# Loads of w_ada issued by ScalarE instead of SyncE, in a decoder layer on one core

## The chip, the cores and the metric

The kernel runs on one core of a Trainium2 chip. The time is device microseconds of one launch. Three runs of the kernel before gave 1894.2, 1889.44 and 1890.69 us, median 1890.69. Engines: PE is TensorE (matmuls; PEld its weight loads), DVE VectorE, ACT ScalarE, POOL GpSimd, SP SyncE, which only issues DMAs here; a q behind an engine's name is its sequencer.

## The reference

One layer on x (1, 256, 4096) float32, with weights w_ada (4096 x 12288), w_in (4096 x 15520) and w_out (4096 x 4096):

```
mod = silu(c) @ w_ada + b_ada ;  shift, scale, gate = split(mod, 3)
h   = rms_norm(x, norm_g) * (1 + scale) + shift
z   = h @ w_in      -> uA, vA, gA, qB, kB, vB, gB, qI, kI, wI
yA  = chunked_sgu(uA, vA)            # gelu, layer_norm, 128x128 mixing per head
yB  = sparse_attention(qB, kB, vB, qI, kI, wI)   # top 64 keys per query, T5 bias
y   = concat(rms_norm(yA) * silu(gA), rms_norm(yB) * silu(gB)) @ w_out
out = x + gate * y
```

c is one vector, so that silu(c) @ w_ada is a product of a vector with a matrix of 201 MB: its cost is reading it.

## The kernel before

Every large product is done in float32 precision by splitting both factors into a high and a low part: a weight tile `raw` (two slices of 128 rows by 512 columns, 512 KB) is copied by ScalarE into high parts `whi` (line 419, two copies), and VectorE (line 425) and GpSimd (line 427) subtract these from `raw` into the low parts `wlo`. PE then multiplies high by high, high by low and low by high (line 457): 12 matmuls of 512 columns for a tile, 10 for the packed tiles of the indexer's queries, where two half products share one matmul.

The stream of weight tiles has 624 entries. First come eight blocks: a block is the four 128-row slices of w_in that belong to 512 features of h, against all columns that are needed early (23 groups of columns, two tiles each: 46 tiles, two of which are narrow, 160 columns). A block's partial products are added to groups in SBUF (line 829). Block b needs its 512 features of h, and these need shift and scale of the same features: a product of silu(c) with 4096 x 2 x 512 values of w_ada, in 32 tiles `wa` of 512 KB. While blocks 0 to 6 are multiplied, this product is made for the next block on VectorE: one `scalar_tensor_tensor` per `wa` tile adds csil[k] times the tile to a sum in PSUM (`ada_gemv`, lines 194 and 196), and `make_h` (lines 324 to 350) makes the features. The first block's product is made ahead of all this (`first_ada`, line 202). After the eighth block come eight visits of 16 tiles for the gate columns of w_in and eight for w_out, and beside them the layer norm, the mixing, the attention, and the product for `gate` (`make_gate`, line 939: 4 x 32 `wa` tiles, and one for the bias).

The order of every engine is the order in which the code is written, step by step. Step t (line 463) loads the raw tile of step t + 3 (`AHEAD`), splits tile t, flushes a delayed read, reads finished sums, lets work beside the stream advance (`tick`) and multiplies tile t. In the first seven blocks `pace(t)` is called ahead of step t and advances `all_h` by as many yields as are due: 33 a block, 32 of them a `wa` tile each.

There are four buffers for raw tiles (`WBUFS`) and two for `wa` tiles. All loads are issued by SyncE, each waiting there until its buffer is free. `ada_gemv` calls `load_ada` right after the operation that read a `wa` tile, so that the next load into that buffer stands in SyncE's order between the raw loads of two steps, and waits for that operation on VectorE.

Of the kernel before, what the change touches and what calls it, by code (L numbers as in the profile page):

```python
# [17 lines left out]
D = 4096  # L18
# [24 lines left out]
def layer(ctx, tc, x, c, w_ada, b_ada, norm_g, w_in, ln_v_g, ln_v_b, w_s, b_s, q_norm_g,  # L43
          k_norm_g, rel_bias, out_norm_a_g, out_norm_b_g, w_out, onehot, out):
    nc = tc.nc
# [20 lines left out]
    def after(read):  # L66
        pending.append(read)

    def flush():
        while pending:  # L70
            pending.pop(0)()

    def misc():
        while len(pending) > 1:
            pending.pop(0)()
        small_ones[0] += 1
        return ms.tile([P, 512], F32, name="ms_ps", tag="ms")

    def small(shape, name):
        return tiny.tile(shape, F32, name=name)  # L80
# [5 lines left out]
    w_ada_t = w_ada[0].rearrange("(k p) (s n) -> p k s n", p=P, s=3)  # L86
# [75 lines left out]
        ada_loads += [(k0, 1, 2, 1, 1024 * i_, 1024) for k0 in list(range(KC)) + [None]]  # L162
    ada_tiles = []

    def load_ada():
        if ada_loads:
            k0, per, s0, ns, d0, width = ada_loads.pop(0)
            wt = wp.tile([P, per, ns, width], F32, name="wa", tag="wa", bufs=2)
            if k0 == "norm":
                for a, src in enumerate((ln_v_g, ln_v_b)):  # L170
                    r = src[0:1, d0:d0 + 512]
                    nc.sync.dma_start(wt[:, 0, 0, a * 512:(a + 1) * 512],
                                      bass.AP(tensor=r.tensor, offset=r.offset, ap=[[0, P], [1, 512]]))
            elif k0 is None:
                nc.sync.dma_start(wt[0:1, 0, 0], b_ada[0:1, 2 * D + d0:2 * D + d0 + width])
            else:
                for kk in range(per):
                    nc.sync.dma_start(wt[:, kk], w_ada_t[:, k0 + kk, s0:s0 + ns, d0:d0 + width])
            ada_tiles.append(wt)

    def ada_gemv(ns, width):

        acc = ap.tile([P, 2, 512], F32, name="acc")
        flat = acc.rearrange("p a b -> p (a b)")
        per = 1024 // (ns * width)
        two = per == 2
        for k0 in range(0, KC, per):
            wt = ada_tiles.pop(0)
            for kk in range(per):
                k = k0 + kk  # L190
                src = wt[:, kk].rearrange("p s w -> p (s w)")
                dst = acc[:, k % 2] if two else flat
                if k < per:
                    nc.vector.tensor_scalar(dst, src, csil[:, k:k + 1], None, op0=OP.mult)
                else:
                    nc.vector.scalar_tensor_tensor(dst, src, csil[:, k:k + 1], dst,  # L196
                                                   op0=OP.mult, op1=OP.add)
            load_ada()
            yield
        return acc  # L200

# [160 lines left out]
    def tick():  # L362
        small_ones[0] = 0
        for b in list(beside):
            b[2] += b[1]
        for b in list(beside):
            if small_ones[0] > 1:
                break
            again = False
            while b[2] >= 1.0:  # L370
                b[2] -= 1.0
                if again:
                    flush()
                again = True
                if next(b[0], "end") == "end":
                    beside.remove(b)
                    break
# [22 lines left out]
    def load_w(t):  # L400
        if t >= len(stream) or t in raws:
            return
        v, i = stream[t]
        nk, w, c0 = min(2, len(v["ks"]) - i), v["w"], v["c0"]
        raw = wp.tile([P, 2, 512], F32, name="raw")
        raw = raw[:, :nk]
        nc.sync.dma_start(raw[:, :, :w], v["src"][:, v["ks"][i]:v["ks"][i] + nk, c0:c0 + w])
        raws[t] = raw
# [3 lines left out]
    def split(t):  # L412

        raw, w = raws.pop(t), stream[t][0]["w"]
        nk = raw.shape[1]
        hi = [sp.tile([P, 512], F32R, name="whi") for _ in range(nk)]
        lo = [sp.tile([P, 512], F32R, name="wlo") for _ in range(nk)]
        for kk in range(nk):
            nc.scalar.activation(hi[kk][:, :w], raw[:, kk, :w], AF.Copy)  # L419
        left = nk * pool_cols[0] * w // 1024 * 2  # L420
        for kk in range(nk):
            cut = w - min(left, w)
            left -= w - cut
            if cut:
                nc.vector.tensor_sub(lo[kk][:, :cut], raw[:, kk, :cut], hi[kk][:, :cut].bitcast(F32))  # L425
            if cut < w:
                nc.gpsimd.tensor_sub(lo[kk][:, cut:w], raw[:, kk, cut:w], hi[kk][:, cut:w].bitcast(F32))  # L427
        halves[t] = hi, lo
# [34 lines left out]
    def step(t):  # L463
        load_w(t + AHEAD)
        due = [v for u, v in reads if u <= t]
        del reads[:len(due)]
        split(t)
        flush()
        for v in due:
            v["read"](v)  # L470
        v, i = stream[t]
        if i == 0 and v["before"]:
            v["before"]()
        tick()
        multiply(t)
        if i + 2 >= len(v["ks"]):
            reads.append((t + 2, v))
# [311 lines left out]
    def norm_v():  # L789

        stats = small([P, NT, 4, 6], "stats")
        for g in range(4):
            z = groups[f"v{g}"]
            nc.scalar.activation(z, z, AF.Gelu_apprx_tanh)
            for n in range(NT):
                nc.vector.bn_stats(stats[:, n, g], z[:, n])
            yield
        mv = small([P, NT, 2], "mv")
        for n in range(NT):
            nc.vector.bn_aggr(mv[:, n], stats[:, n].rearrange("p a b -> p (a b)"))  # L800
        rv = small([P, NT], "rv")
        nc.vector.tensor_scalar(rv, mv[:, :, 1], EPS, None, op0=OP.add)
        nc.gpsimd.tensor_tensor(rv, rv, mhalf.to_broadcast([P, NT]), op=OP.pow)
        for g in range(4):
            z = groups[f"v{g}"]
            rows = ada_tiles.pop(0)[:, 0, 0]
            lg, lb = rows[:, :512], rows[:, 512:]
            for n in range(NT):
                nc.vector.scalar_tensor_tensor(z[:, n], z[:, n], mv[:, n, 0:1], lg,  # L809
                                               op0=OP.subtract, op1=OP.mult)  # L810
            yield
            for n in range(NT):
                nc.vector.scalar_tensor_tensor(z[:, n], z[:, n], rv[:, n:n + 1], lb,
                                               op0=OP.mult, op1=OP.add)
            load_ada()
            yield
        begin_gates()

# [120 lines left out]
    def make_gate(i):  # L939

        acc = yield from ada_gemv(1, 1024)
        tag = ("t4", "k", "vb", "t4")[i]
        accs = (t4 if tag == "t4" else zp).tile([P, 2, 512], F32, name="accs", tag=tag)
        nc.scalar.activation(accs, acc, AF.Copy)
        yield
        fl = accs.rearrange("p a b -> p (a b)")
        nc.vector.tensor_add(fl[0:1], fl[0:1], ada_tiles.pop(0)[0:1, 0, 0])
        load_ada()
        yield
        for a in range(2):  # L950
            hi = s2.tile([P, 512], F32R, name="ghi", tag="s2")
            lo = s2.tile([P, 512], F32R, name="glo", tag="s2")
            nc.scalar.activation(hi, accs[:, a], AF.Copy)
            nc.gpsimd.tensor_sub(lo, accs[:, a], hi.bitcast(F32))
            yield
            m = misc()
            nc.tensor.matmul(m, ones, hi, start=True, stop=False)
            nc.tensor.matmul(m, ones, lo, start=False, stop=True)

            def read(m=m, a=a):  # L960
                nc.scalar.activation(accs[:, a], m, AF.Copy)
                gates[2 * i + a] = accs[:, a]
            after(read)
        yield
# [3 lines left out]
    def all_gates():  # L968
        for i in range(4):
            yield from make_gate(i)  # L970
# [73 lines left out]
    def begin_gates():  # L1044
        nonlocal gat
        gat = later(GATE_STEPS, all_gates(), 234)
# [10 lines left out]
    first_h()  # L1057
    for t in range(AHEAD):
        load_w(t)
    load_ada()  # L1060
    load_ada()
    with tc.manual_schedule():
        for t in range(len(stream)):
            for begin in start.get(t, ()):
                begin()
            if t < last:
                pace(t)
            elif t == last:
                pool_cols[0] = POOL_REST
            step(t)  # L1070
        for _, v in reads:
            v["read"](v)
# [42 lines left out]
```

## Time and profile before

| | |
|---|---|
| three runs, median | 1890.69 us |
| the profiled execution's own time | 1893.78 us |
| its span, first to last instruction | 1892.1 us |
| PE, PEld busy | 1809.0, 1439.2 us |
| DVE, ACT, POOL busy | 1443.7, 933.4, 1299.2 us |
| mean granted TensorE clock | 0.994 |
| HBM read | 536.51 MB |

PE is busy for 96% of the span, but that is no measure of how well it is fed: matmuls overlap in the records, so that a row lasts longer than the distance between two starts. The idle time of PE in a stretch, and the distance of starts where nothing waits, say more. Waits are inferred from semaphores: the row `A <- B` sums the idle time of A's engine that ended when B was done. For SyncE, which is all sequencer, the wait is counted from the end of its last instruction.

### The profile page before, as it was taken

The numbers are of one execution on the slowest core, as the hardware profiler recorded it, in microseconds if no ns is written. First come the engines' busy times: TensorE is split into PE (matmuls) and PEld (weight loads), VectorE is DVE, ScalarE is ACT, GpSimd is POOL, SyncE is SP. The second block draws the span as 40 slices with busy tenths as digits, with TensorE's granted clock in tenths as the row PEclk, the third lists the DMA queues.
The fourth block names the chain that finished last, engine by engine and source line by source line (L and its number), as shares of the span: only waits on it lengthen the run. The fifth ranks groups of instructions, "written<-read, shape, count | busy, mean of one in ns | idle before, by whom it ended". The sixth has DMA issues, their size and how long they took to land.

```text
span 1892.1 us, 27366 instructions
## 1 busy us (share of the span) xinstructions
PE 1809.0 (96%) x8100; PEld 1439.2 (76%) x8100; DVE 1443.7 (76%) x1600; ACT 933.4 (49%) x1716; POOL 1299.2 (69%) x1340
## 2 busy tenths in 40 slices
PE   5798999999999999999999999999999999999998
PEld 2476777777777777787788877788888888888877
DVE  4656788888888888888777888887887577677744
ACT  4356445445454354444455556567654554544443
POOL 0366777777777776777785545767667777877786
PEclk9899999999999999999999999999999999999999
DMA  9899999999999989999975467886788799899974
GB/s 319 316 340 323 314 317 316 318 324 309 341 320 333 319 300 315 329 301 322 311 210 152 132 206 257 267 264 202 245 281 303 248 332 339 294 318 343 320 216 154
DMA packets 269550, 542.53 MB, mean 287 GB/s; under 512 B 17270, under 2 KB 25688, under 8 KB 269404
## 3 DMA queue, kind: packets, MB, share of 16 engines
q1 hardware_dynamic: 269404, 540.79, 84.5%
q8 instruction: 66, 1.08, 0.2%
q14 instruction: 80, 0.66, 0.1%
HBM read 536.51 MB, written 4.22 MB: 286 GB/s over the span
## 4 chain that ended last, share of the span: by engine, by line
PE 45%; DVE 2%; DMA 1%; POOL 1%; ACT 1%; issue 1%; SPq 0%; DVEq 0%; POOLq 0%; ACTq 0%
PE mm_ps L457 38%; PE ms_ps L457 2%; PE ms_ps L573 1%; DMA raw<-in_w_in_dram 1%; DVE wlo L425 1%; PE ms_ps L714 0%; DVE acc L196 0%; POOL wlo L427 0%; PE ms_ps L915 0%; PE ms_ps L867 0%; DVE v L809 0%; PE ms_ps L556 0%; PE ms_ps L742 0%; ACT whi L419 0%; DVE ix L585 0%
## 5 line engine op out<-in xcount | busy, mean ns | idle before, releaser
L427 POOL TENSOR_TENSOR wlo<-raw,whi 128x512 fp32r<-128x512 f32 (+1 forms) x1248 | 1220.8, 1004 | 543.8 <-ACT whi L419 467.0
L419 ACT ACTIVATE whi<-raw 128x512 fp32r<-128x512 f32 (+1 forms) x1248 | 730.9, 618 | 829.9 <-DMA raw<-in_w_in_dram 385.1
L425 DVE TENSOR_TENSOR wlo<-raw,whi 128x320 fp32r<-128x320 f32 (+2 forms) x624 | 636.7, 1022 | 317.3 <-ACT whi L419 200.9
L457 PE MATMUL mm_ps<-whi,hh 128*128 128x512 f32 (+1 forms) x1728 | 566.2, 397 | 19.2 <-ACT whi L419 15.5
L457 PE MATMUL mm_ps<-whi,hl 128*128 128x512 f32 (+1 forms) x1728 | 550.7, 388 | 2.6 <-DVE hl L311 2.6
L457 PE MATMUL mm_ps<-wlo,hh 128*128 128x512 f32 (+1 forms) x1728 | 494.0, 388 | 14.3 <-DVE wlo L425 12.2
L196 DVE SCALAR_TENSOR_TENSOR acc<-wa,csil,acc 128x1024 f32<-128x1024 f32 x341 | 436.4, 1280 | 72.3 <-DMA wa<-in_w_ada_dram 71.2
L457 PEld LDWEIGHTS mm_ps<-whi,hh 128*128 128x128 f32 x1728 | 315.2, 190 | 97.2 <-ACT whi L419 31.0
L457 PEld LDWEIGHTS mm_ps<-wlo,hh 128*128 128x128 f32 x1728 | 320.4, 189 | 86.3 <-POOL wlo L427 12.0
L457 PEld LDWEIGHTS mm_ps<-whi,hl 128*128 128x128 f32 x1728 | 323.8, 189 | 71.0 <-DVE hl L311 2.9
L457 PE MATMUL mm_ps<-whi,yh 128*128 128x512 f32 x448 | 138.1, 389 | 0.0
L457 PE MATMUL mm_ps<-whi,yl 128*128 128x512 f32 x448 | 138.0, 389 | 0.0
L457 PE MATMUL mm_ps<-wlo,yh 128*128 128x512 f32 x448 | 120.2, 390 | 0.6 <-POOL wlo L427 0.6
L457 PE MATMUL mm_ps<-wlo,both 128*128 128x512 f32 x256 | 103.9, 406 | 4.3 <-DVE wlo L425 3.0
L457 PE MATMUL mm_ps<-whi,both 128*128 128x512 f32 x256 | 103.8, 405 | 3.9 <-ACT whi L419 2.8
L457 PEld LDWEIGHTS mm_ps<-wlo,yh 128*128 128x128 f32 x448 | 83.9, 188 | 19.0 <-POOL wlo L427 1.8
L457 PEld LDWEIGHTS mm_ps<-whi,yl 128*128 128x128 f32 x448 | 84.1, 188 | 17.6
L457 PEld LDWEIGHTS mm_ps<-whi,yh 128*128 128x128 f32 x448 | 84.0, 188 | 17.6 <-ACT whi L419 0.2
L457 PEld LDWEIGHTS mm_ps<-wlo,both 128*128 128x128 f32 x256 | 48.0, 187 | 30.7 <-POOL wlo L427 14.5
L829 DVE TENSOR_TENSOR qi<-qi,mm_ps 128x1024 f32<-128x1024 f32 x56 | 67.6, 1207 | 0.0
L457 PEld LDWEIGHTS mm_ps<-whi,both 128*128 128x128 f32 x256 | 48.0, 188 | 23.9 <-ACT whi L419 11.1
L217 PE MATMUL acc<-wa,csil 128*1 128x512 f32 x64 | 28.4, 613 | 10.9 <-DMA wa<-in_w_ada_dram 10.9
(190 smaller groups left out, 1035.5 us busy)
## 6 DMA issues: line engine op xcount, KB each, us to landing
raw<-in_w_in_dram SPq DMA_DIRECT2D x480, 512.0 KB, 5.9
wa<-in_w_ada_dram SPq DMA_DIRECT2D x384, 512.0 KB, 5.0
raw<-in_w_out_dram SPq DMA_DIRECT2D x128, 512.0 KB, 6.0
xs<-in_x_dram SPq DMA_DIRECT2D x8, 512.0 KB, 5.5
xres<-in_x_dram SPq DMA_DIRECT2D x8, 512.0 KB, 7.3
out_dram<-yt SPq DMA_DIRECT2D x16, 256.0 KB, 3.1
raw<-in_w_in_dram SPq DMA_DIRECT2D x16, 160.0 KB, 5.1
wk<-rb_d SPq DMA_DIRECT2D x16, 128.0 KB, 5.6
```

Of the source, the lines that this page charges most:

```text
L196: nc.vector.scalar_tensor_tensor(dst, src, csil[:, k:k + 1], dst, op0=OP.mult, op1=OP.add)
L217: nc.tensor.matmul(acc[g:g + 1, s, :w], csil[:, k:k + 1], wt[:, s], start=i < 4, stop=i >= KC // 2 - 4)
L419: nc.scalar.activation(hi[kk][:, :w], raw[:, kk, :w], AF.Copy)
L425: nc.vector.tensor_sub(lo[kk][:, :cut], raw[:, kk, :cut], hi[kk][:, :cut].bitcast(F32))
L427: nc.gpsimd.tensor_sub(lo[kk][:, cut:w], raw[:, kk, cut:w], hi[kk][:, cut:w].bitcast(F32))
L457: nc.tensor.matmul(v["ps"][n][:, :w], a, b[:, :w], start=n not in begun, stop=i + len(hi) == len(v["ks"]) and j == ends[n])
L573: nc.tensor.matmul(dots[:q, a * S:(a + 1) * S], qt[:, (h0 + a) * q:(h0 + a + 1) * q], kiT[:, :S], start=True, stop=True)
L829: nc.vector.tensor_add(z, z, p)
```

## The change

The DMA engine queue that `load_ada` uses becomes a variable: ScalarE's at first, SyncE's from the step `last` on, with which the eighth block begins. `load_ada` is no longer called right after a `wa` tile is read. Whoever takes a tile (`next_ada`) adds one to a counter, and `load_adas`, called in `step` after `split`, issues as many loads as the counter says; if no tile is left when one is wanted, it issues then. So in the first seven blocks a `wa` load stands in ScalarE's order behind the two high-part copies of the step, and SyncE's order has the raw tiles alone. From the eighth block on, it stands on SyncE behind the raw load of its step.

```
+    to_load = [2]
+    ada_queue = [nc.scalar]
+
     def load_ada():
+        to_load[0] -= 1
         if ada_loads:
+            queue = ada_queue[0]
             k0, per, s0, ns, d0, width = ada_loads.pop(0)
...
-                    nc.sync.dma_start(wt[:, kk], w_ada_t[:, k0 + kk, s0:s0 + ns, d0:d0 + width])
+                    queue.dma_start(wt[:, kk], w_ada_t[:, k0 + kk, s0:s0 + ns, d0:d0 + width])
             ada_tiles.append(wt)
+
+    def load_adas():
+        while to_load[0] > 0:
+            load_ada()
+
+    def next_ada():
+        if not ada_tiles:
+            load_adas()
+        to_load[0] += 1
+        return ada_tiles.pop(0)
...
-            wt = ada_tiles.pop(0)
+            wt = next_ada()
...
-            load_ada()
             yield
...
         split(t)
+        load_adas()
         flush()
...
-    load_ada()
-    load_ada()
+    load_adas()
...
             elif t == last:
                 pool_cols[0] = POOL_REST
+                ada_queue[0] = nc.sync
             step(t)
```

The other two places that take a `wa` tile, in `norm_v` and `make_gate`, are changed in the same way. PE and GpSimd have the same instructions in the same order as before.

SyncE's order in the second block before, where `DMAHW0` to `DMAHW7` are the eight counters of completed loads, each used again by the eighth load after it:

```order
L178 DMA wa<-in_w_ada_dram 128x2x512 [waits DMAHW1_49,DVE_49]
L407 DMA raw<-in_w_in_dram 128x2x512 [waits DMAHW0_49,Pool_49]
L178 DMA wa<-in_w_ada_dram 128x2x512 [waits DMAHW3_49,DVE_49]
L407 DMA raw<-in_w_in_dram 128x2x512 [waits DMAHW2_49,Pool_49]
L178 DMA wa<-in_w_ada_dram 128x2x512 [waits DMAHW6_49,DVE_49]
L407 DMA raw<-in_w_in_dram 128x2x512 [waits DMAHW4_49,Pool_49]
L407 DMA raw<-in_w_in_dram 128x2x512 [waits DMAHW5_49,DVE_49,Pool_49]
```

And SyncE's order in the second to third block now:

```order
L423 DMA raw<-in_w_in_dram 128x2x512 [waits DMAHW0_49,DMAHW6_49,DVE_49,Pool_49]
L423 DMA raw<-in_w_in_dram 128x2x512 [waits DMAHW2_49,DVE_49,Pool_49]
L423 DMA raw<-in_w_in_dram 128x2x512 [waits DMAHW4_49,DVE_49,Pool_49]
L423 DMA raw<-in_w_in_dram 128x2x512 [waits DMAHW3_49,DMAHW5_49,DVE_49,Pool_49]
L423 DMA raw<-in_w_in_dram 128x2x512 [waits DMAHW6_49,DVE_49,Pool_49]
```

The `wa` loads and their waits for VectorE's reads are gone from it; a raw load waits for VectorE and GpSimd, the readers of its buffer, itself.

ScalarE's order in the first seven blocks now, where before it had the `whi` rows alone:

```order
L183 DMA wa<-in_w_ada_dram 128x2x512 [waits DMAHW4_49,DVE_49]
L435 ACTIVATE whi<-raw 128x512 [waits DMAHW5_49,PE_49,Pool_49]
L435 ACTIVATE whi<-raw 128x512 [waits PE_49,Pool_49]
L435 ACTIVATE whi<-raw 128x512 [waits DMAHW6_49,PE_49,Pool_49]
L435 ACTIVATE whi<-raw 128x512 [waits DVE_49,PE_49,Pool_49]
L183 DMA wa<-in_w_ada_dram 128x2x512 [waits DMAHW7_49,DVE_49]
L435 ACTIVATE whi<-raw 128x512 [waits DMAHW0_49,PE_49,Pool_49]
```

A `wa` load comes behind the second copy of the steps that have one, and waits for VectorE.

VectorE's order at the start of the first block before (`md` are the first modulations, `ht` and `hl` h and its low part):

```order
L425 TENSOR_TENSOR wlo<-raw,whi 128x100 [waits DMAHW1_49,Activation_49]
L270 TENSOR_TENSOR md<-ms_ps,cols_152 128x4 [waits PE_49]
L271 TENSOR_TENSOR md<-ms_ps,b_162 128x4
L272 TENSOR_TENSOR md<-md,cols_152 128x4 [waits DVE_49]
L307 TENSOR_SCALAR ht<-xT_204,md 128x256 [waits DVE_49]
L307 TENSOR_SCALAR ht<-xT_204,md 128x256 x3
L194 TENSOR_SCALAR acc<-wa,csil 128x1024 [waits DMAHW3_49]
L311 TENSOR_TENSOR hl_426<-ht,hh_421 128x512 [waits DVE_49,Activation_49]
```

And VectorE's order at the same place now:

```order
L441 TENSOR_TENSOR wlo<-raw,whi 128x100 [waits DMAHW2_49,Activation_49]
L211 TENSOR_SCALAR acc<-wa,csil 128x1024 [waits DMAHW1_49,DVE_49]
L286 TENSOR_TENSOR md<-ms_ps,cols_152 128x4 [waits PE_49]
L287 TENSOR_TENSOR md<-ms_ps,b_162 128x4
L288 TENSOR_TENSOR md<-md,cols_152 128x4 [waits DVE_49]
L323 TENSOR_SCALAR ht<-xT_204,md 128x256 [waits DVE_49]
L323 TENSOR_SCALAR ht<-xT_204,md 128x256 x3
L327 TENSOR_TENSOR hl_426<-ht,hh_421 128x512 [waits DVE_49,Activation_49]
```

The first operation on a `wa` tile (`acc<-wa,csil`) has moved ahead of the first modulations. This is the only instruction of VectorE that stands in another place.

## Rows read from the trace of the kernel before

**Rows 1.** Stretches: us, busy (x count) PE PEld DVE ACT POOL, clock, DMA, GB/s

```profile
70.00:80.00 10.00, 6.99 (x28) 6.49 (x29) 7.71 (x12) 5.13 (x11) 4.93 (x5) 0.50 0.50 169
...
90.00:130.00 40.00, 38.62 (x167) 30.83 (x166) 23.95 (x27) 22.32 (x35) 26.95 (x29) 1.00 0.97 346
130.00:966.00 836.00, 802.01 (x3518) 629.65 (x3517) 682.98 (x694) 388.93 (x696) 613.06 (x619) 1.00 0.92 315
...
1470.00:1650.00 180.00, 179.88 (x801) 149.03 (x802) 127.24 (x117) 90.29 (x153) 139.29 (x139) 1.00 0.89 306
```

**Rows 2.** Timeline of PE: start, us, instruction, count, idle before and releaser

```profile
70.36 0.71 PE L457 MATMUL mm_ps<-whi,hh 128*128 128x160 f32 x2 [1.21 <-ACT hh L278]
...
936.85 1.84 PE L263 MATMUL ms_ps<-one,accs 128*128 128x1 f32 x16
...
966.07 0.35 PE L457 MATMUL mm_ps<-whi,hh 128*128 128x160 f32 x2
...
968.71 0.43 PE L457 MATMUL mm_ps<-whi,both 128*128 128x512 f32 x1
```

**Rows 3.** Chain that ended last, 1400 to 1470 us: start, us, what

```profile
1411.92 43.54 PE mm_ps L457 x192
```

**Rows 4.** Waits, 70 to 966 us: who <- whom, us in total, times, longest

```profile
ACT whi L419 <- DMA raw<-in_w_in_dram: 328.0, 175, 5.0
...
DVE acc L196 <- DMA wa<-in_w_ada_dram: 61.4, 60, 3.4
```

**Rows 5.** Waits of PE, 70 to 966 us

```profile
PE mm_ps L457 <- ACT whi L419: 18.1, 27, 1.7
PE mm_ps L457 <- DVE wlo L425: 13.3, 20, 1.4
```

**Rows 6.** Waits of SyncE's queue, 70 to 966 us

```profile
SPq L178 <- DVE acc L196: 298.0, 148, 5.5
SPq L178 <- DVE wlo L425: 146.5, 67, 4.2
SPq L178 <- DMA wa<-in_w_ada_dram: 107.8, 109, 3.8
```

**Rows 7.** Timeline of ACT, DVE, POOL and SP, 404 to 417 us

```profile
404.57 1.15 ACT L419 ACTIVATE whi<-raw 128x512 fp32r<-128x512 f32 x2 [3.67 <-DMA raw<-in_w_in_dram]
...
405.28 2.10 POOL L427 TENSOR_TENSOR wlo<-raw,whi 128x512 fp32r<-128x512 f32 x2 [2.72 <-ACT whi L419]
...
406.84 1.28 DVE L196 SCALAR_TENSOR_TENSOR acc<-wa,csil,acc 128x1024 f32<-128x1024 f32 x1
...
408.14 0.37 SPq L178 DMA_DIRECT2D wa<-in_w_ada_dram  x1
...
408.60 0.42 SPq L407 DMA_DIRECT2D raw<-in_w_in_dram  x1
...
413.38 0.85 POOL L427 TENSOR_TENSOR wlo<-raw,whi 128x192 fp32r<-128x192 f32 x1
...
414.41 1.15 ACT L419 ACTIVATE whi<-raw 128x512 fp32r<-128x512 f32 x2 [1.93 <-DMA raw<-in_w_in_dram]
414.81 1.28 DVE L196 SCALAR_TENSOR_TENSOR acc<-wa,csil,acc 128x1024 f32<-128x1024 f32 x1
...
416.58 0.42 SPq L407 DMA_DIRECT2D raw<-in_w_in_dram  x1
```

**Rows 8.** DMA issues: what, engine, count, KB each, median us to landing

```profile
raw<-in_w_in_dram SPq DMA_DIRECT2D x480, 512.0 KB, 5.9
wa<-in_w_ada_dram SPq DMA_DIRECT2D x384, 512.0 KB, 5.0
```

**Rows 9.** Timeline of SP and DVE at the start of the first block

```profile
63.86 1.22 SPq L178 DMA_DIRECT2D wa<-in_w_ada_dram  x2
...
69.18 0.16 DVE L270 TENSOR_TENSOR md<-ms_ps,cols 128x4 f32<-128x4 f32 x1 [2.63 <-PE ms_ps L263]
...
70.94 1.28 DVE L194 TENSOR_SCALAR acc<-wa,csil 128x1024 f32<-128x1024 f32 x1
```

More of the change, by code (lines that the diff above doesn't have):

```diff
@@ L171, in load_ada @@
                     r = src[0:1, d0:d0 + 512]
-                    nc.sync.dma_start(wt[:, 0, 0, a * 512:(a + 1) * 512],
+                    queue.dma_start(wt[:, 0, 0, a * 512:(a + 1) * 512],
                                       bass.AP(tensor=r.tensor, offset=r.offset, ap=[[0, P], [1, 512]]))
             elif k0 is None:
-                nc.sync.dma_start(wt[0:1, 0, 0], b_ada[0:1, 2 * D + d0:2 * D + d0 + width])
+                queue.dma_start(wt[0:1, 0, 0], b_ada[0:1, 2 * D + d0:2 * D + d0 + width])
             else:
                 for kk in range(per):
-                    nc.sync.dma_start(wt[:, kk], w_ada_t[:, k0 + kk, s0:s0 + ns, d0:d0 + width])
+                    queue.dma_start(wt[:, kk], w_ada_t[:, k0 + kk, s0:s0 + ns, d0:d0 + width])
             ada_tiles.append(wt)
+    def load_adas():
[6 more added lines that the diff above has]
+        return ada_tiles.pop(0)
     def ada_gemv(ns, width):
@@ L805, in norm_v @@
             z = groups[f"v{g}"]
-            rows = ada_tiles.pop(0)[:, 0, 0]
+            rows = next_ada()[:, 0, 0]
             lg, lb = rows[:, :512], rows[:, 512:]
@@ L946, in make_gate @@
         fl = accs.rearrange("p a b -> p (a b)")
-        nc.vector.tensor_add(fl[0:1], fl[0:1], ada_tiles.pop(0)[0:1, 0, 0])
-        load_ada()
+        nc.vector.tensor_add(fl[0:1], fl[0:1], next_ada()[0:1, 0, 0])
         yield
@@ L1059, in layer @@
         load_w(t)
-    load_ada()
-    load_ada()
+    load_adas()
     with tc.manual_schedule():
```

## The prediction

> **What bounds the kernel now.** I read the stages first, then TensorE's (PE's) own pace, then who waits for whom in the stage that falls short of it, and last the order of time inside one such wait.
>
> The stretch table shows where anything is to be had. In the first seven blocks of the input projection PE is idle 34 us of the 836 shown (802.01 busy), with the DMA engines at a share of 0.92 and 315 GB/s; in the gates it is busy 179.88 of 180 at 306 GB/s [rows 1]. The projection's main matmuls run from 70.36 to 966.07 us [rows 2], 895.7 us for seven blocks of 46 weight tiles: 2.78 us a tile. PE's pace without a wait is 43.54 us for 192 matmuls, 0.2268 us each [rows 3]. A block has 16 packed tiles of 10 and 28 of 12 wide matmuls, 496 x 0.2268 = 112.5 us, then 968.71 - 966.07 = 2.6 us for the narrow ones and 1.8 us for the sums of modulations [rows 2]: 117 us, 2.54 us a tile, 819 us for seven. So 77 us of the stage are stalls. Some 8 of them belong to its start, where the granted clock is 0.50, the lower level of 1.2 GHz, from 70 to 80 us [rows 1], after PE had waited for the first h.
>
> Who waits: ScalarE's high parts (whi) waited for a raw weight tile 175 times, 328.0 us in all, and VectorE's modulation step (line 196, called gemv below) waited for its w_ada tile 60 times, 61.4 us [rows 4]. PE itself shows 18.1 us over 27 waits for whi and 13.3 us over 20 for VectorE's low parts (wlo) [rows 5]. A matmul row counts 0.39 us against a pace of 0.227, so each wait is understated by 0.16 us: 22.4 and 16.5 us, 39 together; the other 30 are gaps too short for a row.
>
> Why raw tiles are late: SyncE's queue stands before a w_ada load 298.0 + 146.5 + 107.8 us, 552 of the 896 [rows 6], and the next raw load stands behind it. One instance in full: whi at 404.57, the tile's buffer free when GpSimd ends at 405.28 + 2.10 = 407.38, but gemv runs from 406.84 to 408.12, the w_ada load goes at 408.14 and the raw load at 408.60: 1.2 us after its buffer was free [rows 7]. Another buffer was free at 413.38 + 0.85 = 414.23 and its load went at 416.58, 2.35 us late [rows 7]. Four raw buffers make a loop: 4 x 2.78 = 11.1 us = whi to free 2.8 + lateness 1.2 to 2.4 + landing 5.9 [rows 7, 8] + what is left, about 0.6, ScalarE's other waits. This loop and not PE paces the stage.
>
> **The change part by part.** *The raw loads stand alone on SyncE in the first seven blocks.* The lateness goes; the loop becomes 2.8 + 5.9 + 0.6 = 9.3 us, 2.3 us a tile, under PE's 2.54. The mean wait of whi is 328.0/175 = 1.9 us [rows 4] and 1.2 to 2.4 us is taken off in front of it; I take 1.5, three quarters of the waits' time. Of the 22.4 us in which PE stood for whi that gives back 17. Bounds: nothing, if the landing grows by what the issue gains; 22.4.
>
> *VectorE's part.* wlo is late to PE when whi was late, which goes, or when gemv was stuck on w_ada before it, which stays. I take half of 16.5, 8 us; bounds 0 and 16.5. Of the short gaps I take 2 of 30.
>
> *ScalarE issues 228 loads (224 of w_ada, 4 of the norm rows).* On SyncE such an issue takes 0.37 us [rows 7]; on ScalarE no row here shows one. From below it is 0, from above 228 x 0.37 = 84 us, all on the path. ScalarE is busy only 389 of 836 us in this stage [rows 1], and PE holds up to two split tiles, so that I take it as hidden; were the cover gone, the 84 us would count.
>
> *The wait it adds.* The load waits for the gemv that frees its buffer, and the next tile's whi, then GpSimd's wlo, queue behind it. The gemv at 414.81 ends at 416.09 and would hold ScalarE, whose whi pair from 414.41 ends at 415.56, for 0.5 us [rows 7]. After such a gemv VectorE needs 1.2 us for its wlo of the same tile, ScalarE 0.4 + 0.6 us for the issue and the first whi of the next, and PE has the wlo matmuls to do meanwhile, so nearly all of it is covered. I take 2 us of loss; it would be up to 16.5 if the present VectorE stalls doubled.
>
> *The w_ada loads are later, not earlier.* Now the load goes 0.02 us after gemv's end (408.12 to 408.14); then it goes after the whi pair of that step if that ends later, up to 1.15 us. Two buffers make the second loop: gemv 1.28 + landing 5.0 [rows 8] + issue 0.4 = 6.7 us; at PE's pace 32 loads a block leave 2 x 117/32 = 7.3 us. The slack is 0.6 us, which is why not all stalls go.
>
> *Start.* The first gemv moves ahead of the first modulation md on VectorE and must wait for the first w_ada tile. That load went at 63.86; 5.0 to land and 1.28 give 70.1 against md at 69.18, but h's low part no longer waits for that gemv (70.94 + 1.28) [rows 9]. Loss taken 1 us, bounds 0 and 2.
>
> *From the last block on* SyncE carries both again, with the w_ada load behind the raw load of its step instead of ahead of it. PE was never short of a tile in the gates, where this happens most, 179.88 us busy of 180 [rows 1]: taken as 0, bounds 3 either way. The eight completion counters are now shared by two queues; one is reused eight loads later, over 11 us, when a landing takes 5.9: nothing.
>
> Sum: -17 - 8 - 2 + 2 + 1 = -24 us. The profiled execution took 1893.78 us, so it would take 1870; the runs shown have a median of 1890.69, and I predict 1867. About 0.3%, 6 us, is what a measurement of this kernel can tell from no change.
>
> **The rivals.** *A: the landing pays it back.* The same bytes go over the same 16 engines, already at a share of 0.92. If a raw load issued 1.5 us earlier finds one more load ahead of it, 0.524 MB at the 346 GB/s of the best stretch [rows 1], it lands 1.5 us later and the loop is as long as before. Gain 0 to 6, say 3: 1888. Against it: the gates run free of stalls at 306 GB/s, and the stage's 281 MB (308 wide and 14 narrow raw tiles, 224 of w_ada) take 813 us at 346 GB/s, no more than PE's 819; and each raw load already has a w_ada load just ahead of it, so its 5.9 us hold those bytes.
> The Trainium skill, page "DMA: Bandwidth & Descriptors", section "Issuing engines are not separate DMA queues", says that starting DMAs on several engines "will only save the time on the sequencer it takes to initiate the DMA, which is usually small". By that rule alone the gain would be this rival's. The trace shows something beside it: SyncE's 552 us are not spent on issuing but on standing in order before w_ada loads that were not yet allowed.
>
> *B: ScalarE is held and the w_ada loop binds (slower).* Each load goes later by the issue and a whi pair, 0.4 + 1.15 = 1.55 us at most. The loop of two is now 2 x 895.7/224 = 8.0 us, of which 1.28 + 5.0 leave 1.7 in which VectorE is not yet there. If the raw loads, no longer held back, also lengthen the w_ada landing, the loop grows as soon as that lengthening is over 0.15 us on all loads; at 0.3 it is 0.15 a loop, 0.075 a load, and 224 x 0.075 = 17 us, with ScalarE, VectorE and GpSimd held at once: 1908. For it: 60 gemvs already wait. Against it: whi will come earlier than now, so the full pair is seldom added.
>
> *C: the stage becomes PE's own.* All 39 us of waits and a dozen of the short gaps go: 1890.69 - 50 = 1841. Against it: VectorE is itself busy 683 of 836 us [rows 1], and gemv, addition and low part often fall on one tile.
>
> **How the numbers follow.** Forecast 0.56, A 0.18, B 0.13, C 0.13. Half of what the forecast takes is 1879, all of its upper bounds (22.4 + 16.5) 1852; that is its own range. To hold 8 in 10 I go on to 1843 below, short of C, and to 1895 above, past A and short of B. Faster by over 0.3%: the forecast, C and a quarter of A, 0.73; within 0.3%: the rest of A, 0.14; slower: B, 0.13.
>
> **What would show it.** In the changed profile whi's wait for raw in 70 to 966 us should fall from 328 us to under 120, SyncE should wait only for low parts, and the last block's narrow matmuls should start near 943 instead of 966 us, with 322 to 325 GB/s in the stage. gemv's wait for w_ada may grow, to 60 to 120 us. I am wrong if whi's wait stays near 300 with a raw landing over 7 us (A), if whi waits for VectorE or the issue while gemv's wait goes past 150 us (B), or if the start of the last block moves while the end does not.

## The result and the profile after

The changed kernel is slower. Its median is 1922.18 us (four runs, 1916.83 to 1923.48), that of the kernel before in the same rounds 1891.62 us: a ratio of 1.0156, 95% interval 1.0132 to 1.0179. 1867 us was forecast, and 1895 was the upper end of the range. The profiled execution after took 1922.79 us, its span is 1921.1.

**Where the time went.** First the stretches of the kernel after, to be read against [rows 1] (length, then busy us of PE, PEld, DVE, ACT and POOL, granted clock, DMA share, GB/s):

```profile
130.00:966.00 836.00, 789.36 (x3405) 616.64 (x3404) 641.93 (x675) 368.14 (x667) 575.11 (x598) 0.98 0.92 310
1470.00:1650.00 180.00, 180.00 (x808) 149.24 (x807) 133.81 (x123) 91.72 (x150) 131.44 (x134) 1.00 0.89 305
```

PE is busy 789.36 us of the 836, where it was 802.01, and the rate has fallen from 315 to 310 GB/s, while 322 to 325 was forecast. The gates are as before. PE's timeline after gives the two ends of the stage, against [rows 2]:

```profile
71.36 0.71 PE L473 MATMUL mm_ps<-whi,hh 128*128 128x160 f32 x2 [1.21 <-ACT hh L294]
...
996.41 0.35 PE L473 MATMUL mm_ps<-whi,hh 128*128 128x160 f32 x2
```

The stage begins 1.0 us later (70.36 before) and the last block 30.3 us later (966.07 before). From there to the end of the span it is 1921.1 - 996.41 = 924.7 us, before 1892.1 - 966.07 = 926.0. So all of the loss lies in the first seven blocks, and the return of the loads to SyncE in the eighth costs nothing.

**Who waits now.** Waits of the kernel after from 70 to 966 us (who <- whom: us in total, times, longest), against [rows 4]:

```profile
ACT whi L435 <- DVE wlo L441: 237.0, 78, 5.7
POOL wlo L443 <- ACT whi L435: 180.0, 127, 7.8
DVE acc L213 <- DMA wa<-in_w_ada_dram: 131.5, 89, 5.9
...
ACT whi L435 <- DMA raw<-in_w_in_dram: 4.7, 3, 2.1
```

and those of PE alone, against [rows 5]:

```profile
PE mm_ps L473 <- DVE wlo L441: 38.8, 32, 5.1
...
PE mm_ps L473 <- ACT whi L435: 10.4, 23, 0.8
```

The raw tiles are no longer late: 4.7 us of waits instead of 328.0. In their place ScalarE stands 237.0 us for VectorE, gemv's wait for w_ada has more than doubled (131.5 against 61.4), and PE's wait for VectorE's low parts has gone from 13.3 to 38.8 us. SyncE waits for low parts alone, against [rows 6]:

```profile
SPq L423 <- DVE wlo L441: 683.5, 310, 8.8
SPq L423 <- POOL wlo L443: 76.1, 177, 0.5
```

One instance in full, from the timeline of ACT, DVE and POOL after (start, us, engine and line, what; in brackets the idle time ahead and what ended it):

```profile
409.08 0.37 ACTq L183 DMA_DIRECT2D wa<-in_w_ada_dram  x1
409.58 1.15 ACT L435 ACTIVATE whi<-raw 128x512 fp32r<-128x512 f32 x2 [0.61 <-PE mm_ps L473]
...
414.61 1.29 DVE L213 SCALAR_TENSOR_TENSOR acc<-wa,csil,acc 128x1024 f32<-128x1024 f32 x1 [3.31 <-DMA wa<-in_w_ada_dram]
415.81 0.48 DVE L441 TENSOR_TENSOR wlo<-raw,whi 128x320 fp32r<-128x320 f32 x1
415.93 0.37 ACTq L183 DMA_DIRECT2D wa<-in_w_ada_dram  x1
416.43 2.19 ACT L435 ACTIVATE whi<-raw 128x512 fp32r<-128x512 f32 x4 [5.69 <-DVE wlo L441]
...
417.13 3.37 POOL L443 TENSOR_TENSOR wlo<-raw,whi 128x512 fp32r<-128x512 f32 x3 [4.69 <-PE mm_ps L473]
```

A w_ada load goes at 409.08 and gemv gets it at 414.61, after 3.31 us of waiting. ScalarE has ended its pair at 410.73 and has the next w_ada load in front of it, whose buffer that gemv frees: it goes at 415.93, and only then whi, after 5.69 us of idling, and GpSimd after 4.69. The page names the last semaphore (VectorE's wlo, 415.81) as releaser of whi; what held ScalarE is the load ahead of it. One late w_ada tile stops VectorE, ScalarE and GpSimd together, and PE runs dry:

```profile
416.44 0.70 PE L473 MATMUL mm_ps<-wlo,hh 128*128 128x512 f32 x2 [1.05 <-DVE wlo L441]
```

**Why w_ada is late.** The DMA issues from 130 to 900 us (what, engine, count, KB, median us from issue to landing), before and then after:

```profile
raw<-in_w_in_dram SPq DMA_DIRECT2D x267, 512.0 KB, 6.4
wa<-in_w_ada_dram SPq DMA_DIRECT2D x197, 512.0 KB, 5.3
```

```profile
raw<-in_w_in_dram SPq DMA_DIRECT2D x258, 512.0 KB, 5.3
wa<-in_w_ada_dram ACTq DMA_DIRECT2D x191, 512.0 KB, 6.0
```

The raw landing became shorter by 1.1 us, the w_ada landing longer by 0.7. The packets say in which part. This table is worked out from the packets and instructions of the traces (means in us from 130 us to the end of the seventh block, where the views above give medians; a load has landed when its semaphore is set, which is what gemv waits for; "hold": ScalarE is kept until gemv has ended; the stage ends with the start of the last block):

```
                              w_ada load:                                          tile    stage
                              issue to     issue to     first to     issue to      period  ends at
                              first packet last packet  last packet  landing
before                        1.98         3.93         1.95         5.22          2.76     966.07
after                         1.80         5.15         3.35         5.72          2.85     996.41
one queue, no hold            2.41         4.21         1.80         5.35          2.61     921.41
one queue, hold               2.33         4.16         1.83         5.36          2.66     941.67
one queue, longer hold        2.31         4.18         1.87         5.34          2.68     949.19
two queues, one step later    1.74         5.14         3.40         5.65          2.86     997.65
one queue, one step later     2.91         4.92         2.00         5.72          3.00    1044.71
```

From the end of gemv to the issue of the next load it is 0.03 us before and after: the load isn't later. It starts no later either (1.80 against 1.98 us), but its packets take 3.35 us instead of 1.95, and those of a raw load 2.70 instead of 1.91: the loads of the two queues share the 16 engines. The landing grows by less than the transfer, 0.50 us in the mean, because 1.3 us passed between the last packet and the landing before and 0.6 us pass now. The rows below the second are experiments.

**The clock.** Before, the granted clock is 1.00 from 90 to 966 us [rows 1]. After, it is at 0.50, the lower level of 1.2 GHz, in seven stretches between 128 and 774 us, 27.2 us together, each at or right behind a stretch of 1.6 to 5.1 us in which PE stood idle. One of them, which falls into a wait of 2.35 us for VectorE's low part, in the columns of the stretches above:

```profile
504.00:510.80 6.80, 6.46 (x15) 4.71 (x16) 6.61 (x7) 3.45 (x6) 4.73 (x5) 0.50 0.84 267
```

So a part of the loss, by an estimate at most half of the 27.2 us, is the price of the waits in clock, and not the waits themselves.

### The profile page after: what moved, and what is told of

It reads as the page before. It is cut to its first block, busy times and chain, and to the rows that moved or that the text cites. A ratio compares the mean times of both kernels' runs of the same rounds, so it can differ in the third digit from the quotient of the medians.

```text
span 1921.1 us, 27617 instructions
## 1 busy us (share of the span) xinstructions
PE 1821.7 (95%) x8100; PEld 1447.1 (75%) x8100; DVE 1426.0 (74%) x1600; ACT 934.3 (49%) x1716; POOL 1277.4 (66%) x1340
## 5 line engine op out<-in xcount | busy, mean ns | idle before, releaser
L443 POOL TENSOR_TENSOR wlo<-raw,whi 128x512 fp32r<-128x512 f32 (+1 forms) x1248 | 1199.8, 987 | 594.3 <-ACT whi L435 450.8
L441 DVE TENSOR_TENSOR wlo<-raw,whi 128x320 fp32r<-128x320 f32 (+2 forms) x624 | 620.4, 995 | 288.7 <-ACT whi L435 154.1
```

## The experiments

Two theories at first: the loss is ScalarE held at the load (H), or it is the longer landing of w_ada, brought about by raw loads that are no longer held back (L). When L as put had fallen, the second queue itself took its place (Q), against the time that ScalarE spends on issuing (I). Each kernel was timed in three rounds beside the kernel before.

### One queue, no hold

The changed kernel with one line other, so that the w_ada load stands on SyncE behind the raw load of its step:

```diff
-    ada_queue = [nc.scalar]
+    ada_queue = [nc.sync]
```

> The changed kernel with the w_ada loads on SyncE throughout, still issued after the split of a step, so behind that step's raw load. ScalarE is never held. Theory H (ScalarE, held until the gemv ends, makes whi late): the 30 us go and more, since the next raw load needs the same VectorE order anyway: 1860 to 1885, with whi's wait for raw in the first seven blocks well under the 328 us of before. Theory L (raw loads that are issued on time lengthen the landing of the w_ada loads, whose loop of two buffers then binds): raw loads are still on time and the w_ada loads still share the engines with them, so 1905 to 1925 and gemv's wait for w_ada over 120 us.

Measured: 1847.12 us, ratio 0.9771 (0.9741 to 0.9801). It leaves out nothing of the reference and is faster than both kernels, and than either theory had it. Waits from 70 to 940 us, with those of SyncE's queue last, then that stretch, and PE's timeline at the start of its last block:

```profile
ACT whi L435 <- DMA raw<-in_w_in_dram: 146.6, 93, 3.8
...
DVE acc L213 <- DMA wa<-in_w_ada_dram: 123.2, 101, 3.9
...
PE mm_ps L473 <- DVE wlo L441: 10.6, 17, 2.2
```

```profile
SPq L183 <- DVE wlo L441: 184.3, 109, 3.6
SPq L183 <- DVE acc L213: 119.5, 106, 2.9
SPq L183 <- DMA wa<-in_w_ada_dram: 95.2, 82, 3.3
```

```profile
70.00:940.00 870.00, 852.88 (x3853) 700.45 (x3854) 684.29 (x755) 450.41 (x768) 658.08 (x676) 0.99 0.95 330
```

```profile
921.41 0.35 PE L473 MATMUL mm_ps<-whi,hh 128*128 128x160 f32 x2
```

L's forecast falls: with raw tiles that come sooner (whi waits 146.6 us for them instead of 328.0), at 330 GB/s, w_ada's transfer is no longer than before (1.80 us). It is no full test of L, since raw loads are still held back in part: SyncE stands 399 us before w_ada loads, where it stood 552 [rows 6]. gemv still waits 101 times, 123.2 us, nearly as long as in the changed kernel, and PE hardly feels it (10.6 us for VectorE), since ScalarE and GpSimd go on meanwhile. The order of the loads alone is worth 1890.69 - 1847.12 = 43.6 us.

### One queue, with the hold

To that kernel a one-element copy on ScalarE where the load stood, which reads the sum that gemv writes; no DMA on ScalarE:

```diff
+    last_acc = [None]
...
     def load_adas():
+        held = to_load[0] > 0 and last_acc[0] is not None and pool_cols[0] == POOL_EARLY
         while to_load[0] > 0:
             load_ada()
+        if held:
+            nc.scalar.activation(ssx[0:1, 0, 0:1], last_acc[0][0:1, 0, 0:1], AF.Copy)
...
+            last_acc[0] = acc
```

> The kernel with all loads on SyncE, issued after the split (1847 us), and where ScalarE would have issued a w_ada load it now copies one element of the sum that the gemv has just written, so that it is held until the gemv ends and issues no DMA; one queue. Theory H2 (the hold is what costs: whi of the next tile, and GpSimd behind it, stop together with VectorE whenever a gemv waits for its w_ada tile): 1900 to 1920, PE's wait for wlo in the first seven blocks back from 11 us to over 30. Theory Q (the second queue is what costs: its loads take turns with the raw loads and land later, 5.67 us against 5.27): 1847 to 1860, with the wait for wlo under 20 us. If both matter, in between, and its distance from 1847 is the hold's share.

Measured: 1868.15 us, ratio 0.9890 (0.9868 to 0.9913). Waits from 70 to 940 us, and PE's timeline at the start of its last block:

```profile
ACT ssx L195 <- DVE acc L218: 371.5, 208, 6.0
...
DVE acc L218 <- DMA wa<-in_w_ada_dram: 103.6, 74, 3.4
...
PE mm_ps L479 <- DVE wlo L447: 17.6, 18, 2.8
```

```profile
941.67 0.35 PE L479 MATMUL mm_ps<-whi,hh 128*128 128x160 f32 x2
```

The time lies between the two theories' ranges, and PE's wait for wlo rose to 17.6 us, not past 30. ScalarE stands 371.5 us in 208 waits, more than in the changed kernel (there its idle time just ahead of the loads, summed from the instructions in the same window, is 262 us at 183 loads), and that costs 1868.15 - 1847.12 = 21 us; the intervals of the two ratios leave this some 7 us either way. The hold is a cost, but it explains neither the slower time nor the landing: w_ada's transfer is 1.83 us.

### The same with the issue time

Three copies for each load instead of one, 0.48 us, above the 0.37 us that an issue takes on ScalarE:

```diff
             nc.scalar.activation(ssx[0:1, 0, 0:1], last_acc[0][0:1, 0, 0:1], AF.Copy)
+            nc.scalar.activation(ssx[0:1, 0, 1:2], last_acc[0][0:1, 0, 1:2], AF.Copy)
+            nc.scalar.activation(ssx[0:1, 0, 2:3], last_acc[0][0:1, 0, 2:3], AF.Copy)
```

> As the run in which ScalarE copies one element of the sum instead of issuing the load (1868 us, one copy 0.16 us), with three such copies, 0.48 us, more than the 0.37 us that a DMA issue takes on ScalarE. One queue, no DMA on ScalarE. Theory Q (what is left between 1868 and the changed kernel's 1922 is the second queue: a w_ada tile shares the engines with the raw tiles and takes 3.4 us instead of 1.8 to be moved): 1868 to 1880. Theory I (it is ScalarE's time for 228 issues): 1900 to 1925.

Measured: 1873.83 us, ratio 0.9905 (0.9869 to 0.9941). I falls: the issue time is worth some 6 us, which the intervals of the two ratios (some 8 us either way) don't tell from nothing. This kernel has the order of the loads, the hold and the time on ScalarE of the changed one, and is 1922.18 - 1873.83 = 48 us faster, also some 8 either way; the one without the issue time is 54 us faster. What is left between them is the queue on which the loads go, with what comes of it: the two transfers overlap, and the raw loads no longer stand behind w_ada loads.

### A third w_ada buffer, on two queues and on one

Room for it is made by adding the fourth group of `u` into the buffer of the third, so that the three kernels with this buffer don't compute the reference's output:

```diff
-    t4 = ctx.enter_context(tc.tile_pool(name="t4", bufs=5))
+    t4 = ctx.enter_context(tc.tile_pool(name="t4", bufs=4))
...
-    to_load = [2]
+    to_load = [3]
...
-            wt = wp.tile([P, per, ns, width], F32, name="wa", tag="wa", bufs=2)
+            wt = wp.tile([P, per, ns, width], F32, name="wa", tag="wa", bufs=3)
...
-        groups[f"u{g}"] = t4.tile([P, NT, 512], F32, name=f"u{g}", tag="t4")
+        groups[f"u{g}"] = t4.tile([P, NT, 512], F32, name=f"u{g}", tag="t4") if g < 3 else groups["u2"]
```

`first_ada` has its two `wa` buffers made three in the same way.

> The changed kernel with a third w_ada buffer. The room for it comes from adding the fourth group of u to the third one's buffer (the output is not the reference's). Loads are still on ScalarE, which is still held until the gemv that frees the buffer. Theory L: the loop has three buffers, gemv's wait for w_ada falls from 131 to under 30 us in the first seven blocks, and the time to 1860 to 1880. Theory H: gemv's wait falls too, but ScalarE's hold stays, and the time stays at 1905 or more.

> Three w_ada buffers and all loads on SyncE, issued after the split (the fourth group of u is added to the third one's buffer, so the output is not the reference's). Against the same with the loads on ScalarE (1831) and on ScalarE a step later (1826). Theory Q: one queue lets w_ada loads land sooner, but with three buffers nobody waits for them: 1822 to 1831. Theory H2: no hold: 1822 to 1828, 3 to 8 us under ScalarE's 1831. Over 1840 would mean that the second queue itself helps when there is a buffer more.

Measured: two queues 1830.88 us, ratio 0.9687 (0.9657 to 0.9717); one queue, with `ada_queue = [nc.sync]` beside it, 1823.43 us, 0.9647 (0.9629 to 0.9664). The first is faster than both theories had it, the second within the ranges of both. Waits of the first of them from 70 to 940 us, then gemv's wait from 130 to 890:

```profile
ACT whi L435 <- DVE wlo L441: 95.5, 45, 3.8
...
PE mm_ps L473 <- DVE wlo L441: 1.1, 4, 0.5
```

```profile
DVE acc L213 <- DMA wa<-in_w_ada_dram: 4.9, 8, 0.9
```

The loads are still issued by ScalarE and their median landing is 6.3 us, longer than the 6.0 of the changed kernel, but a w_ada tile now comes in time and ScalarE's 95.5 us no longer reach PE. The pair also shows what the second queue does when both kernels load at nearly the same rate (342 and 344 GB/s from 130 to 890 us): a w_ada transfer takes 3.30 us on two queues and 1.73 on one, and the landing 6.29 and 5.92 us in the mean. Hold and second queue together cost 7 us here, at the edge of what the two intervals tell, where they cost 75 us with two buffers (1922.18 - 1847.12). So the loss is made in the loop of two w_ada buffers.

### The load one step later

The counter is passed on by one step, so that a load should find its buffer free: with three buffers on ScalarE, with two on ScalarE, with two on SyncE. By the lines left out here, a load goes without the delay from the last block on.

```diff
+    owed_loads = [0]
+
+    def load_adas_late():
...
+            for _ in range(min(owed_loads[0], to_load[0])):
+                load_ada()
+        owed_loads[0] = to_load[0]
...
-        load_adas()
+        load_adas_late()
```

> As the run with three w_ada buffers, and each load on ScalarE is issued one step later, when the gemv that frees its buffer is long done, so that ScalarE is not held. Both theories: 1850 to 1875. Theory H: more than 10 us faster than three buffers without the delay. Theory L: the same as that within 6 us.

> The changed kernel with its two w_ada buffers, each load on ScalarE issued one step (about 2.7 us) later: no hold of ScalarE, but a longer loop. Theory H: faster than the changed kernel by more than 15 us, under 1905. Theory L: the loop of two grows by up to 2.7 us, 1.3 us for each of 224 loads if nothing absorbs it, so slower than the changed kernel: 1950 to 2200, and gemv waits for nearly every w_ada tile.

> Two w_ada buffers, each load issued one step later as in the run on ScalarE that took 1921 us, but on SyncE's queue. Nobody but SyncE waits for it. Theory Q: a load comes later but moves at full rate, 1.8 us instead of 3.4: 1845 to 1880, at least 40 us under 1921. Without an effect of the second queue the longer loop alone would give 1900 to 1921.

Measured: three buffers 1826.23 us, ratio 0.9665 (0.963 to 0.97), under the range of both theories; it is 5 us under the same without the delay, which the intervals don't tell from nothing, as theory L had it. Two buffers on ScalarE 1921.17 us, ratio 1.0162 (1.013 to 1.0194), the same as the changed kernel; both expectations missed it. It was meant to take the hold away at two buffers, and did so only in part, since ScalarE runs ahead: its waits from 70 to 940 us still show

```profile
DVE acc L223 <- DMA wa<-in_w_ada_dram: 178.0, 105, 5.1
...
ACT whi L445 <- DVE wlo L451: 85.2, 44, 4.0
...
PE mm_ps L483 <- DVE wlo L451: 46.2, 43, 2.5
```

Held a third as long (85.2 against 237.0 us), it is no faster. The loads now go 0.31 us behind gemv's end in the mean; by the price found below that is an estimate of some 20 us, about what the shorter hold could give back, but no run takes the two apart. The transfer is 3.40 us as in the changed kernel.

Two buffers on SyncE took 1971.7 us, ratio 1.0433 (1.0394 to 1.0472), and the expectation of 1845 to 1880 missed by 90. The load now goes 1.21 us after gemv's end, behind a raw load just issued (it lands after 5.72 us instead of 5.35):

```profile
DVE acc L223 <- DMA wa<-in_w_ada_dram: 232.5, 158, 3.8
...
PE mm_ps L483 <- DVE wlo L451: 69.8, 55, 3.3
```

The miss is useful: it gives the price of the loop. From gemv's end to the landing it became 1.2 + 0.4 = 1.6 us longer, and the kernel 1971.7 - 1847.12 = 125 us: about 80 us for each microsecond that is added to the round of a w_ada load. In a loop of two that is never early, 224 loads would make it 112 us. On an estimate from these two prices, the 5.72 - 5.34 = 0.38 us by which a load of the changed kernel lands later than one of the kernel with the longer hold are worth 30 to 43 us, against 48 to 54 measured. The clock may be the rest: it is at 0.50 for 20 us more than in the kernel with the longer hold (27.2 against 6.8 us from 90 us to the start of the last block), at most 10 us by the half; it also enters the price itself, with 54 us at 0.50 in the kernel of 1971.7 us and none in the one of 1847.12. No run takes it apart.

## Why the prediction was wrong

Taken together, by steps of one thing each (the names are those of the table above):

```
before                                              1890.7
raw loads less late, w_ada behind the raw      -43  1847.1   one queue, no hold
ScalarE held until gemv ends                   +21  1868.2   one queue, hold
its time for the issue                          +6  1873.8   one queue, longer hold
loads on the second queue                      +48  1922.2   after
```

- **What bounds the kernel, and the raw loads alone on SyncE: right.** whi's wait for raw fell from 328.0 to 4.7 us and SyncE waits for low parts alone, both as forecast. The gain of 27 us (17 + 8 + 2) was too small: the one-queue kernel gained 43 with raw loads that still waited in part, so more of the gaps too short for a row seem to have belonged to late raw tiles than the 2 us that I took.
- **"The w_ada loads are later, not earlier": this step failed, and it carries the most.** The load was not later at all (0.03 us after gemv's end, as before). I priced the loop of two with the landing of before, 5.0 us [rows 8], and found 0.6 us of slack at PE's pace. That landing is the median of the whole kernel; in this stage it was 5.3 us, which holds the 0.4 us of the issue already, so the sum hardly changes. But a landing belongs to the queue on which it was measured: on a second queue the load's transfer took 3.35 us instead of 1.95, and its landing 5.72 us instead of 5.22 in the mean. And the slack of 0.6 us is a mean that a single loop does not have: the order of VectorE shows that between two uses of a buffer there are mostly three tiles of the stream, but two in 53 of 206 loops, 5.1 us at PE's 2.54 a tile, where gemv and landing alone take 1.28 + 5.22. Those 53 had 37 of the 48 us that gemv stood ahead of its operation before (130 to 966 us); in the trace after the loops with three tiles wait too, 42 us instead of 8. The sum has no term for it; it is 48 to 54 us.
- **"The wait it adds": 2 us, bounds to 16.5: this step failed too.** By itself it costs 21 us, some 27 with the issue, in the kernels with one queue. My working took a gemv that was on time, as the one at 414.81 [rows 7], where the hold is 0.5 us; in the trace after the holds that count stand behind gemvs that wait for their load, 5.69 us in the instance above. "Half of VectorE's stalls stay" could not bound what happens when three engines stop at once.
- **Issue on ScalarE, start, tail: right.** An issue takes 0.37 us there, 84 us in all, and some 6 of them are felt, with an interval that includes none. The start cost 1.0 us, as taken (the first narrow matmul at 71.36 against 70.36), the tail nothing (924.7 against 926.0).
- **The rivals.** A fell: the raw landing became shorter, and the raw waits went. C's time was near the one-queue kernel's, not the changed one's. B had the place, the direction and the mark by which to know it, except that gemv's wait is 131.5 us and not past 150; it was priced at 17 us with a growth of the landing of 0.3 us, worked out from nothing, where the mean shows 0.50 and the median 0.7, and it came with the second queue: on one queue the landing stayed at 5.34 to 5.36 us with the hold, and with three buffers at the same rate it is the second queue that adds 0.37. Its chance of 0.13 and the range's end at 1895 were too low: the row against it, whi coming earlier, says nothing on the landing, and the 60 gemvs that already waited [rows 4] said that many of its loops had nothing left.

The Trainium skill, page "DMA: Bandwidth & Descriptors", section "Queues, rings and completion order", says that each DMA engine takes turns packet by packet between the queues that have work for it. The trace agrees: the share of the engines hardly moves (0.92 before and after), the w_ada transfer goes from 1.95 to 3.35 us and that of a raw load from 1.91 to 2.70. In the prediction I cited that page's section "Issuing engines are not separate DMA queues" for a second queue that brings nothing but issue time; here it brought less than nothing, 48 us.

What stays open: no run has two buffers and a second queue without any hold, so the 48 us are the second queue's given the hold; the run meant for it still held ScalarE for 85 us. How the two add up without it wasn't measured. Nor does a run with two queues keep the raw loads back, so that the overlap of the transfers and the freedom of the raw loads can't be told apart within the 48 us.

## What to carry to other kernels

A load that waits for its buffer at the head of a queue holds back every load behind it: put it behind those that are already allowed, in the same queue, before thinking of a second one. A landing time holds for the queue and the neighbours with which it was measured; before loads of a loop with few buffers move to another queue, price the loop with a longer landing (here the transfer went from 1.8 to 3.4 us and the landing up by 0.4), and take its slack from the shortest round, not from the mean. If its reader already waits in the profile, most of what is added to the round is paid: here 80 of at most 112 us for each microsecond. With few buffers, an engine that computes should not issue a load whose buffer is freed by a reader that itself waits for loads (21 us here with two; with three, hold and second queue together cost 7).

## What was not expected of the hardware

- A second queue nearly doubled the transfer of a w_ada load, from 1.73 to 3.30 us with three buffers and from 1.87 to 3.35 with two, and added only 0.37 and 0.38 us to its mean landing. The raw landing, which fell from 6.4 to 5.3 us in the median, owes that to the order of the loads: it is 5.4 us in the kernel with one queue and the longer hold.
- With the same loads in another order, SyncE's queue alone moved 339 GB/s instead of 319 from 130 to 900 us.
- The granted clock fell to 0.50 seven times in the changed kernel's stage, each time at an idle stretch of PE, for 27.2 us together; in the same stage of the kernel before and of the one with one queue and no hold it did not fall after 90 us.
- An issue took 0.37 us on ScalarE, as on SyncE.
